# Order of reuse of SBUF buffers: the age of a release in ticks instead of in releases

## The chip, the cores and the metric

The kernel runs on one core of one Trainium2 chip. The metric is the device time of one execution in microseconds (us). A run repeats it and gives the median; two versions are compared by runs on the same chip.

## The reference

One inference step of a two-layer decoder in float32: 1024 prompt tokens and 8 decode tokens, model width 2048. Cut to what matters:

```
def pool_layer(x, prefix, pos, ...):                 # mixer A
    z = x @ w_in                                     # 2048 -> 4096
    u, gate = z[..., :D_POOL], z[..., D_POOL:]
    d, new_state = multiscale_pool(u, prefix, pos)   # trailing windows 2/4/8/16, minus u
    d = einsum('btgc,gce->btge', d, w_grp) * scale   # four groups of 512
    y = (d * silu(gate)) @ w_out
    return layer_norm(ALPHA * x + y), new_state

k, v = shared_kv(x)                                  # once, 4 KV heads of 64, partial rotary

def attn_layer(x, pos, kb, vb, ...):                 # mixer B
    z = x @ w_in
    q, gate = rope(z[..., :D_ATTN]), z[..., D_ATTN:]
    o = attn_core(q, kb, vb, ..., sinks)             # window 128, 32 heads, a sink per head
    y = (o * silu(gate)) @ w_out
    return layer_norm(ALPHA * x + y)
```

## The kernel before

**Tiling.** The tokens form two chunks (512 and 520 columns). The four big projections are the phases `ai`, `ao` (mixer A, in and out) and `bi`, `bo` (mixer B). Each phase treats its product as a two-by-two block product and needs, instead of eight block products, seven (`idx` 0 to 6) on sums of blocks, in the groups A (0, 5), C (1, 3, 6) and B (2, 4). Every operand is split in two: a high part rounded to fp32r, cast by ACT (weights L399, activations L613), and the rest, subtracted by DVE (weights L407, activations L619). PE then runs three matmuls for each 128 x 128 block, high by high, high by low and low by high (L784, L785, L786), of 260 or 512 columns. Sums of weight blocks are DVE's L443; some go to DRAM by POOL's queue and come back by SP's. L894, L896, L915, L924 and L954 move accumulators between PSUM and SBUF, POOL's L882 and L907 store parts of them, SP's L949 loads one part back. Between the projections stand the pooling, the attention (L1859 to L1987: scores L1880, mask L1900, exponentials L1915, transposes L1933, values L1962, the gate's activation L2028) and the layer norms.

**Ticks.** `plan` lists all units of work and gives each a tick; `self.i` is the tick that is being written, from -30 in the opening to some 800 at the end, and a tick holds 24 matmuls of 260 columns or 12 of 512. A load is put on the calendar 11 ticks ahead of its use (`L_LOAD`), a cast is due 5 ticks ahead, a subtraction 4 (`L_LOW`). Tasks without a fixed tick go when ACT and DVE have time by the planner's meters (`gentle`). `x_tick` starts loads of activations, and looks at how many buffers are free.

**Buffers.** `Mem` holds 53 SBUF buffers of 128 x 1040 floats, each usable whole or as two halves. `full` and `half` hand out the free one with the smallest number in `f`, which `release` wrote when the buffer came back. The number counts releases (`clock`, one more with each). A buffer whose content a DMA still has to store is given back at once with 10 added (`free(True)`), so that it is taken later. `half` takes a free half of a split buffer, unless that half came back within the last 6 releases and over 7 whole buffers are free; then it splits a whole one. The choice is made while the program is written: it sets no wait itself, but the new owner's first instruction waits on the chip until the old owner's last readers (engine or store) are done.

**Order.** `in_order` fixes the order of PE, ACT and DVE to that of the source. SP's loads and POOL's stores and memsets are ordered by the framework, and their place in the queue depends on the buffers that they take. Every queue runs in order: an instruction that waits holds all behind it.

Of the kernel before, what the change touches and what calls it, by code (L numbers as in the profile page):

```python
# [93 lines left out]
class Slot:  # L94


    def __init__(self, mem, i, h, a):
        self.mem, self.i, self.h, self.a = mem, i, h, a
# [9 lines left out]
        return self.r[:, : k * n].rearrange("p (k n) -> p k n", k=k)  # L108

    def free(self, stored=False):  # L110
        self.mem.release(self, 10 if stored else 0)


class Mem:


    def __init__(self, pool, n):
        self.pool = pool
        self.t = [None] * n
        self.f = [[0, 0] for _ in range(n)]  # L120
        self.clock = self.n = 0

    def new(self, i):
        self.n += 1
        self.t[i] = self.pool.tile([P, 2 * TMAX], F32, tag=f"m{i}", name=f"m{i}_{self.n}")
# [9 lines left out]

    def half(self):
        part = [(a if b is None else b, i) for i, (a, b) in enumerate(self.f) if (a is None) != (b is None)]
        if part and min(part)[0] > self.clock - 6 and len(self.whole()) > 7:
            part = []
        i = min(part)[1] if part else min(self.whole(), key=lambda i: max(self.f[i]))  # L140
        h = 0 if self.f[i][0] is not None else 1
        if not part:
            self.new(i)
        self.f[i][h] = None
        return Slot(self, i, h, self.t[i][:, h * TMAX : (h + 1) * TMAX])

    def release(self, s, late):
        self.clock += 1
        for h in (0, 1) if s.h is None else (s.h,):
            assert self.f[s.i][h] is None  # L150
            self.f[s.i][h] = self.clock + late


class Unit:
# [6 lines left out]
class Kern:  # L161
    def __init__(self, ctx, tc, io):
        self.tc, self.io = tc, io
        self.nc = tc.nc
        pool = lambda name, **kw: ctx.enter_context(tc.tile_pool(name=name, **kw))
        one = pool("one", bufs=1)
        self.smp = pool("smp", bufs=2)
        dram = pool("dram", bufs=1, space=bass.MemoryType.DRAM)
        self.psd = [pool(f"psd{i}", bufs=1, space=bass.MemoryType.PSUM) for i in range(3)]
        self.pso = pool("pso", bufs=1, space=bass.MemoryType.PSUM)  # L170
        self.four = None
        ctx.callback(self.use_four, None)
        self.prm = one.tile([P, N_PRM], F32, name="prm")
        self.cst = one.tile([P, N_CST], F32, name="cst")
        self.mki = one.tile([P, P], I32, name="mki")
        self.nsink = one.tile([P, NH], F32, name="nsink")
        self.carry = one.tile([P, NK, NST], F32, name="carry")
        self.kdec = one.tile([P, 2, NDEC], F32, name="kdec")
        self.qdt = one.tile([P, 256], F32, name="qd")
        self.qd = [  # L180
            self.qdt[:, i * P : (i + 1) * P].rearrange("p (b j t) -> p b j t", b=NDEC, j=2) for i in range(2)
        ]
        self.sgd = [one.tile([P, 8, NDEC], F32, name=f"sgd{i}") for i in range(2)]
        self.jr = one.tile([P, P], F32R, name="jr")[:]
        self.mem = Mem(pool("mem", bufs=1), NSLOT)
        self.n = self.ring = self.turns = 0
        self.lastO = -99
        self.i = -99
        self.cal, self.posts, self.side, self.tasks = {}, [], [], []
        self.seen, self.stepped, self.clock = 0, -9, {"p": 0.0, "v": 0.0, "a": 0.0}  # L190
        dr = lambda n, s: dram.tile(s, F32, tag=n, name=n)
        self.Td, self.act, self.n0, self.bb, self.ws = {}, {}, {}, {}, {}
        for ph in PH:
            n = INP[ph]
            self.Td[n] = dr(f"t{n}", [P, 8, 4, TMAX])
            for c in range(2):
                self.act[n, c] = io[f"x{c}"] if n == "x" else dr(f"{n}{c}", [P, NK, TMAX])
            self.n0[ph] = dr(f"n{ph}", [P, len(POS[ph]), TMAX])
            self.bb[ph] = dr(f"b{ph}", [P, len(POS[ph]), 2, TMAX])
            self.ws[ph] = [dr(f"s{ph}{p}", [P, 2, 1024]) for p in range(len(POS[ph]))]  # L200
        for c in range(2):
            self.act["p", c] = dr(f"p{c}", [P, NK, TMAX])
# [496 lines left out]
    def x_tick(self):  # L699
        free = lambda: len(self.mem.whole())  # L700
        n = 0
        for k in self.xl[:12]:
            far = self.x_at(k) - self.i
            if far > X_FAR or n > 1:
                break
            if self.x_ready(k, X_LAG if k[1] not in TROW and far > X_URGE else 0) and (
                (len(self.xraw) < 4 and free() > X_SPARE + 2) or (far <= X_LOAD and free() > 3) or far <= X_LOAD - 4
            ):
                self.x_load(k)
                n += 1  # L710
# [1776 lines left out]
```

## Time and profile before

| what | value |
|---|---|
| time, median of three runs | 2275.03 us (2274.45 to 2277.27) |
| the profiled execution's own time | 2273.81 us |
| its span, first to last instruction | 2272.0 us |
| mean granted PE clock | 0.999 |
| matmuls | 17312 |
| read from and written to HBM | 371.88 and 171.16 MB |
| loads of weights (L384, L435), 512 KB each, median from issue to landing | 5.0 to 7.0 us |

An engine's busy time is the time in which it executes; issuing a DMA or waiting is not counted. A row of the timeline has the start in us, the time in us, engine, line, operation and tiles; `x2` merges two that follow each other, and square brackets give the engine's idle time before and what ended it. SPq is SP's queue of DMA issues. In the trace's names the buffers' numbers are left out: `m` is any of the 53.

### The profile page before, as it was taken

Reading aid. Unit: us, or ns where it says so; the run is one execution under the profiler, and the core shown is the slowest. Engines: PE = TensorE matmul, PEld = TensorE weight load, DVE = VectorE, ACT = ScalarE, POOL = GpSimd, SP = SyncE. Lnnn points to the kernel's source line nnn. Section 1 sums busy time; section 2 is a strip of 40 time slices with the busy share of each in tenths; the row PEclk is TensorE's granted clock in tenths of the full one; section 3 lists DMA queues with packets and bytes.
Section 4 is the critical chain, followed back from the end, with each engine's and each line's share of the span. In section 5 each row is a group of like instructions: output and inputs, shape, how many; then the busy total and the mean of one; then the engine's idle time right before and its main releaser. Section 6 shows DMA issues by size and latency. Waiting matters only on the chain.

```text
span 2272.0 us, 42903 instructions
## 1 busy us (share of the span) xinstructions
PE 2262.4 (100%) x17312; PEld 2130.5 (94%) x17312; DVE 1598.4 (70%) x2009; ACT 1136.1 (50%) x2372; POOL 197.8 (9%) x418
## 2 busy tenths in 40 slices
PE   9999999999999999999999999999999999999998
PEld 7889999999999899999888899999999998889998
DVE  7667746746667587685786876666566879687688
ACT  6344333343334443454576644545647678553365
POOL 0101001100100111000011010101000000111000
PEclk9999999999999999999999999999999999999999
DMA  9859757673657898888488776666754556898873
GB/s 305 314 209 350 233 213 256 227 249 117 243 184 261 276 336 291 292 304 297 153 295 301 245 244 205 230 195 220 244 169 124 177 189 224 284 356 304 301 250 132
DMA packets 190262, 556.43 MB, mean 245 GB/s; under 512 B 26096, under 2 KB 31600, under 8 KB 190064
## 3 DMA queue, kind: packets, MB, share of 16 engines
q1 hardware_dynamic: 147936, 401.82, 54.0%
q0 software_dynamic: 41984, 151.61, 17.4%
q8 instruction: 135, 2.21, 0.4%
q14 instruction: 63, 0.52, 0.1%
q10 hardware_dynamic: 144, 0.27, 0.0%
HBM read 371.88 MB, written 171.16 MB: 239 GB/s over the span
## 4 chain that ended last, share of the span: by engine, by line
PE 96%; DVE 2%; ACT 1%; DMA 0%; issue 0%; SPq 0%; ACTq 0%; DVEq 0%
PE pD L784 28%; PE pD L786 28%; PE pD L785 28%; PE pD L1351 4%; PE pO L1962 2%; PE pS L1880 2%; PE pS L1933 1%; PE pD L848 1%; DVE m L619 0%; DMA m<-in_wia 0%; DVE m L407 0%; PE pO L848 0%; DMA m<-in_x 0%; PE pO L2087 0%; DVE m L1693 0%
## 5 line engine op out<-in xcount | busy, mean ns | idle before, releaser
L784 PE MATMUL pD<-m,m 128*128 128x260 f32 (+1 forms) x4736 | 1428.6, 302 | 0.4 <-ACT m L894 0.4
L786 PE MATMUL pD<-m,m 128*128 128x260 f32 (+1 forms) x4736 | 1420.7, 300 | 0.0
L785 PE MATMUL pD<-m,m 128*128 128x260 f32 (+1 forms) x4736 | 1420.2, 300 | 0.2 <-DVE m L619 0.2
L784 PEld LDWEIGHTS pD<-m,m 128*128 128x128 f32 x4736 | 891.7, 188 | 38.8 <-issue 5.5
L786 PEld LDWEIGHTS pD<-m,m 128*128 128x128 f32 x4736 | 891.4, 188 | 32.7
L785 PEld LDWEIGHTS pD<-m,m 128*128 128x128 f32 x4736 | 891.8, 188 | 31.9 <-DVE m L619 0.6
L407 DVE TENSOR_TENSOR m<-m,m 128x1024 fp32r<-128x1024 f32 x358 | 435.1, 1218 | 144.2 <-ACT m L399 118.9
L399 ACT CAST m<-m 128x1024 fp32r<-128x1024 f32 x358 | 373.0, 1045 | 48.4 <-DVE m L443 11.7
L443 DVE TENSOR_TENSOR m<-m,m 128x1024 f32<-128x1024 f32 x200 | 243.8, 1219 | 10.4 <-DMA m<-in_woa 2.5
L915 ACT COPY m<-pD 128x260 f32<-128x260 f32 (+1 forms) x126 | 56.0, 444 | 306.4 <-PE pD L786 306.0
L619 DVE TENSOR_TENSOR m<-m,m 128x1040 fp32r<-128x1040 f32 x108 | 130.0, 1234 | 24.1 <-ACT m L613 11.8
L924 ACT ACTIVATE m<-pD 128x260 f32<-128x260 f32 x100 | 38.7, 387 | 180.8 <-PE pD L786 172.7
L926 DVE TENSOR_TENSOR m<-pD,m 128x260 f32<-128x260 f32 x100 | 42.6, 426 | 113.0 <-PE pD L786 109.8
L613 ACT CAST m<-m 128x1040 fp32r<-128x1040 f32 x108 | 111.2, 1061 | 14.6 <-DVE m L407 6.7
L1915 ACT ACTIVATE m<-m,sm 128x128 f32<-128x128 f32 x256 | 99.2, 392 | 0.0
L1351 PE MATMUL pD<-m,m 128*128 128x260 f32 (+1 forms) x576 | 91.5, 319 | 0.0
L1351 PEld LDWEIGHTS pD<-m,m 128*128 128x128 f32 x576 | 82.0, 188 | 8.3
L896 ACT COPY m<-pD 128x260 f32<-128x260 f32 x68 | 25.6, 377 | 124.9 <-PE pD L786 124.9
L1945 DVE TENSOR_TENSOR m<-m,cst 128x1024 f32<-128x1024 f32 x32 | 39.1, 1221 | 69.0 <-ACT m L1941 68.7
L1928 ACT ACTIVATE m<-m,sm 128x128 f32<-128x128 f32 x256 | 81.8, 395 | 7.1 <-DVE sm L1923 7.1
L881 ACT ACTIVATE m<-pD 128x512 f32<-128x512 f32 x50 | 29.8, 597 | 99.4 <-PE pD L786 90.6
L894 ACT ACTIVATE m<-pD 128x260 f32<-128x260 f32 x68 | 26.4, 388 | 101.3 <-PE pD L786 101.3
(246 smaller groups left out, 1857.1 us busy)
## 6 DMA issues: line engine op xcount, KB each, us to landing
m<-in_wib SPq DMA_DIRECT2D x96, 512.0 KB, 5.0
m<-in_wia SPq DMA_DIRECT2D x94, 512.0 KB, 5.6
m<-in_woa SPq DMA_DIRECT2D x48, 512.0 KB, 6.2
m<-in_wob SPq DMA_DIRECT2D x48, 512.0 KB, 7.0
sbi<-m POOLq DMA_DIRECT2D x36, 512.0 KB, 4.2
m<-sbi SPq DMA_DIRECT2D x36, 512.0 KB, 4.5
m<-in_x SPq DMA_DIRECT2D x32, 520.0 KB, 7.4
sai<-m POOLq DMA_DIRECT2D x32, 512.0 KB, 3.9
```

The costliest lines, as they stand in the source:

```text
L399: self.nc.scalar.copy(e["hi"].r[:, :1024], e["raw"].a[:, :1024])
L407: self.nc.vector.tensor_sub(o.r[:, :1024], s.a[:, :1024], e["hi"].a[:, :1024])
L443: self.nc.vector.tensor_add(s[o].a[:, :1024], s[a].a[:, :1024], s[b].a[:, :1024])
L613: self.nc.scalar.copy(h.r[:, : 2 * TMAX], s.a[:, : 2 * TMAX])
L619: self.nc.vector.tensor_sub(o.r[:, : 2 * TMAX], s.a[:, : 2 * TMAX], h.a[:, : 2 * TMAX])
L784: nc.tensor.matmul(ps[:, :w], wh[:, s], h, start=new and n2 == 0, stop=False, skip_group_check=on)
L785: nc.tensor.matmul(ps[:, :w], wh[:, s], l, start=False, stop=False, skip_group_check=on)
L786: nc.tensor.matmul(ps[:, :w], wl[:, s], h, start=False, stop=n2 == 7, skip_group_check=on)
L915: self.evac(ph, pos)(self.dest(ph, pos, m, 0)(cs), ps[:, : cs.stop - cs.start])
L1351: nc.tensor.matmul(ps[:, : cs.stop - cs.start], ws[:, s], d[:, cs], start=f0 and k == 0, stop=l0 and k == 3,)
L1915: nc.scalar.activation(x["s3"][:, i, :], x["s3"][:, i, :], AF.Exp, bias=nm[:, i : i + 1], scale=0.125, accum_out=rs[:, i : i + 1],)
L1928: nc.scalar.activation(x["s3"][:, i, :], x["s3"][:, i, :], AF.Copy, scale=rs[:, i : i + 1])
```

## The change

A release is no longer numbered by the count of releases but by the tick in which it is written (`self.i`, which `Kern` hands to `Mem` as `tick`). `clock` now grows by 0.001 a release and only keeps the order within a tick. The handicap of a buffer that is still to be stored is 3.5 ticks instead of 10 releases; a half counts as fresh within 2 ticks instead of 6 releases. Before the first tick `tick` is negative, so buffers that come back in the opening now stand ahead of those never used, whose number is 0.

```diff
--- before.py
+++ after.py
@@ -108,7 +108,7 @@
         return self.r[:, : k * n].rearrange("p (k n) -> p k n", k=k)
 
     def free(self, stored=False):
-        self.mem.release(self, 10 if stored else 0)
+        self.mem.release(self, 3.5 if stored else 0)
 
 
 class Mem:
@@ -119,6 +119,7 @@
         self.t = [None] * n
         self.f = [[0, 0] for _ in range(n)]
         self.clock = self.n = 0
+        self.tick = lambda: 0
 
     def new(self, i):
         self.n += 1
@@ -135,7 +136,7 @@
 
     def half(self):
         part = [(a if b is None else b, i) for i, (a, b) in enumerate(self.f) if (a is None) != (b is None)]
-        if part and min(part)[0] > self.clock - 6 and len(self.whole()) > 7:
+        if part and min(part)[0] > self.tick() + self.clock - 2 and len(self.whole()) > 7:
             part = []
         i = min(part)[1] if part else min(self.whole(), key=lambda i: max(self.f[i]))
         h = 0 if self.f[i][0] is not None else 1
@@ -145,10 +146,10 @@
         return Slot(self, i, h, self.t[i][:, h * TMAX : (h + 1) * TMAX])
 
     def release(self, s, late):
-        self.clock += 1
+        self.clock += 0.001
         for h in (0, 1) if s.h is None else (s.h,):
             assert self.f[s.i][h] is None
-            self.f[s.i][h] = self.clock + late
+            self.f[s.i][h] = self.tick() + self.clock + late
 
 
 class Unit:
@@ -183,6 +184,7 @@
         self.sgd = [one.tile([P, 8, NDEC], F32, name=f"sgd{i}") for i in range(2)]
         self.jr = one.tile([P, P], F32R, name="jr")[:]
         self.mem = Mem(pool("mem", bufs=1), NSLOT)
+        self.mem.tick = lambda: self.i
         self.n = self.ring = self.turns = 0
         self.lastO = -99
         self.i = -99
```

No engine gets an instruction more or less. PE's order is the same throughout. Lines of the changed file stand two lower down in what follows (L2028 is L2030). In a name such as `m47_1964_21174` 47 is the buffer, 1964 counts the whole buffers handed out, and the last number counts all tiles.

First place: ACT in the attention of the last phase, at 1900 to 1910 us of the trace; ahead of the change

```order
L1915 ACTIVATE m42_1945_21047,sm_2857_21097<-m42_1945_21047,sm_2855_21095 128x128 x4
L2028 ACTIVATE m52_1963_21173<-m8_1932_20782 128x1040
L1941 COPY m6_1965_21202<-pS_2248_11329 128x1024
L1915 ACTIVATE m42_1945_21047,sm_2857_21097<-m42_1945_21047,sm_2855_21095 128x128 x4
L399 CAST m4_1968_21212<-m14_1944_20972 128x1024
L1896 COPY m2_1971_21255<-pS_2248_11329 128x1024
```

and now

```order
L1917 ACTIVATE m30_1946_21048,sm_2857_21098<-m30_1946_21048,sm_2855_21096 128x128 x4
L2030 ACTIVATE m47_1964_21174<-m34_1933_20783 128x1040
L1943 COPY m35_1966_21203<-pS_2248_11329 128x1024
L1917 ACTIVATE m30_1946_21048,sm_2857_21098<-m30_1946_21048,sm_2855_21096 128x128 x4
L401 CAST m10_1969_21213<-m37_1945_20973 128x1024
L1898 COPY m41_1972_21256<-pS_2248_11329 128x1024
```

with these rows of DVE at the same place of the changed program:

```order
L621 TENSOR_TENSOR m7_1955_21117<-m49_1886_20173,m26_1905_20437 128x1040
L621 TENSOR_TENSOR m38_1956_21119<-m47_1925_20708,m19_1948_21056 128x1040
L928 TENSOR_TENSOR m39_1940_20911<-pD_2847_20913,m31_1922_20702 128x260
L1865 TENSOR_TENSOR m36_1953_21108<-m35_1898_20330,m36_1953_21108 128x512
L409 TENSOR_TENSOR m9_1961_21168<-m33_1929_20751,m15_1942_20935 128x1024
L621 TENSOR_TENSOR m46_1962_21170<-m51_1931_20755,m42_1957_21121 128x1040
L621 TENSOR_TENSOR m49_1963_21172<-m10_1932_20757,m0_1958_21123 128x1040
```

The order is the same; L2030 (before L2028) now writes buffer 47, which the subtraction L621 into buffer 38 reads, and the cast L401 (before L399) writes buffer 10, read by L621 into buffer 49.

Second place: ACT some 90 us on, at 1993 to 2005 us, where attention tiles are split for `bo`. `qd` holds the decode columns that L611 copies into a tile ahead of its cast; ahead of the change

```order
L613 CAST m22_2064_22113<-m38_2033_21859 128x1040
L399 CAST m42_2066_22131<-m3_2048_22043 128x1024
L915 COPY m46_2059_22102<-pD_2912_21976 128x512
L611 COPY m0_2047_21993<-qd_81 128x2x8
L613 CAST m40_2068_22152<-m0_2047_21993 128x1040
L881 ACTIVATE m23_2072_22187<-pD_2922_22156 128x512
L1433 ACTIVATE m2_2075_22197<-m46_2059_22102 128x1024
```

and now

```order
L615 CAST m8_2066_22115<-m11_2035_21861 128x1040
L613 COPY m1_2047_21977<-qd_81 128x2x8
L615 CAST m31_2067_22118<-m1_2047_21977 128x1040
L401 CAST m44_2069_22136<-m25_2050_22045 128x1024
L917 COPY m37_2061_22104<-pD_2912_21979 128x512
L883 ACTIVATE m11_2071_22154<-pD_2922_22159 128x512
L1435 ACTIVATE m16_2077_22199<-m37_2061_22104 128x1024
```

The pair of copy and cast that stood behind the weight's cast (L399, now L401) and the copy out of PSUM (L915, now L917) stands ahead of them.

Third place: SP's queue from 1985 to 2008 us. `in_wob` are weights, `to` are sums of attention tiles, `h0` and `h1` are the residual of the two chunks, `nbo` is a stored part of an accumulator; ahead of the change

```order
L435 DMA m35_2060_22104<-in_wob 128x1024
L1379 DMA m37_2070_22169<-h0_121 128x2x512
L949 DMA m10_1951_21101<-nbo_146 128x520
L435 DMA m34_2073_22191<-in_wob 128x1024
L603 DMA m13_2078_22203<-to_143 128x2x512
L603 DMA m52_2069_22154<-to_143 128x2x512
L435 DMA m47_2074_22193<-in_wob 128x1024
L603 DMA m43_2092_22263<-to_143 128x2x512
L960 DMA m30_2079_22218<-h1_122 128x2x520
L435 DMA m45_2080_22220<-in_wob 128x1024
L603 DMA m1_2084_22231<-to_143 128x2x512
L603 DMA m7_2085_22233<-to_143 128x2x512
```

and now

```order
L437 DMA m29_2062_22106<-in_wob 128x1024
L605 DMA m15_2072_22157<-to_143 128x2x512
L1381 DMA m43_2073_22172<-h0_121 128x2x512
L951 DMA m11_2071_22154<-nbo_146 128x520
L437 DMA m10_2075_22193<-in_wob 128x1024
L437 DMA m6_2076_22195<-in_wob 128x1024
L962 DMA m12_2081_22220<-h1_122 128x2x520
L605 DMA m25_2080_22205<-to_143 128x2x512
L437 DMA m50_2082_22222<-in_wob 128x1024
L605 DMA m7_2085_22230<-to_143 128x2x512
L605 DMA m19_2086_22232<-to_143 128x2x512
L437 DMA m38_2087_22249<-in_wob 128x1024
```

One load of `to` (now into buffer 15) has moved ahead of those of `h0` and `nbo`, another (buffer 25) from ahead of weights and `h1` to behind them, and a third, which wrote buffer 43 ahead of the change, has gone behind these rows.

## Prediction

> **What bounds the kernel now.** I read the page first (busy shares, chain of waits), then PE's own waits, then a table of stretches, then the order of the changed program against the trace.
>
> ```profile
> span 2272.0 us, 42903 instructions
> PE 2262.4 (100%) x17312; PEld 2130.5 (94%) x17312; DVE 1598.4 (70%) x2009; ACT 1136.1 (50%) x2372; POOL 197.8 (9%) x418
> PE 96%; DVE 2%; ACT 1%; DMA 0%; issue 0%; SPq 0%; ACTq 0%; DVEq 0%
> ```
>
> PE is busy for 2262.4 of 2272.0 us, and it makes 96% of the chain that ended last. Nothing in this change takes a matmul away or adds one, so what it can give is bounded by the 9.6 us in which PE idles. Where these lie is in the table of stretches (each row: length, then busy us and count of each engine, granted clock, DMA share, GB/s), and what ended the longest of them is in the list of PE's waits (total, times, longest):
>
> ```profile
> 0.00:57.00 57.00, 54.83 (x233) 43.94 (x234) 44.34 (x60) 34.12 (x49) 5.03 (x23) 1.00 0.92 305
> 57.00:1881.00 1824.00, 1822.95 (x14107) 1725.65 (x14106) 1248.63 (x1554) 888.94 (x1898) 159.77 (x334) 1.00 0.70 239
> 1881.00:1938.00 57.00, 56.92 (x463) 50.28 (x461) 49.81 (x73) 48.30 (x134) 5.39 (x11) 1.00 0.66 227
> 1938.00:1995.00 57.00, 56.71 (x393) 46.12 (x393) 35.47 (x56) 29.98 (x70) 7.27 (x14) 0.97 0.84 292
> 1995.00:2052.00 57.00, 57.00 (x373) 52.09 (x372) 52.89 (x53) 26.86 (x41) 7.10 (x14) 1.00 0.97 343
> 2052.00:2109.00 57.00, 57.00 (x478) 57.00 (x477) 43.09 (x48) 19.90 (x32) 7.38 (x13) 1.00 0.87 300
> ...
> 2215.00:2272.00 57.00, 50.99 (x395) 49.63 (x393) 46.98 (x84) 32.77 (x65) 0.00 (x0) 0.99 0.37 133
> ```
>
> ```profile
> PE pO L2198 <- POOL m L880: 1.0, 1, 1.0
> PE pD L735 <- ACT m L2234: 0.7, 1, 0.7
> PE pO L1807 <- ACT m L924: 0.5, 1, 0.5
> PE pD L784 <- ACT m L894: 0.4, 1, 0.4
> PE pO L1962 <- DVE m L2108: 0.3, 1, 0.3
> ```
>
> 57.00 - 54.83 = 2.2 us are the opening and 57.00 - 50.99 = 6.0 us the closing normalisation. Between 57 and 2215 us PE idles 1.05 + 0.08 + 0.29 = 1.4 us in all. The waits behind that are for the copy of an accumulator, an attention value, a decode column: none is a wait for a buffer. So today the buffers cost PE nothing, and a better order of reuse has 1.4 us to win.
>
> **The change, part by part.** First, its size. The second number in a buffer's name counts the whole buffers handed out; the cast that the trace has at 1994.6 us writes the 2069th (second place shown with the change). That is 2069 / 1994.6 = 1.04 per us, and about as many come back, so ten releases, the old handicap of a stored buffer, are some 9.6 us. A tick is 24 matmuls of 260 columns; the row from 2052 us above gives 57 / 478 = 0.119 us for one, so a tick is 2.9 us and 3.5 ticks are 10 us (estimates from these rows). On average the two rules say the same; they differ where releases come in bursts.
>
> Instructions added or removed: none on any engine. What moves is (1) which buffer each instruction takes, hence which earlier reader it waits for; (2) the place of some twenty ACT and eight DVE instructions between 1994 and 2029 us; (3) the order of SP and POOL. I took each wait of the changed order and looked up in this trace whether the awaited reader had ended when the waiting instruction started. PE has no wait that would be late. Some ACT instructions, one group on DVE and some SP loads have. The largest of each kind follow.
>
> (1a) The gate's activation at 1902 us (first place shown with the change). It now writes buffer 47, which the second split of the DVE pair at L619 still reads.
>
> ```profile
> 1902.36 1.07 ACT L2028 ACTIVATE m<-m 128x1040 f32<-128x1040 f32 x1
> 1903.33 1.00 ACT L1941 COPY m<-pS 128x1024 f32<-128x1024 f32 x1
> ...
> 1905.77 1.04 ACT L399 CAST m<-m 128x1024 fp32r<-128x1024 f32 x1
> 1908.67 1.02 ACT L1896 COPY m<-pS 128x1024 f32<-128x1024 f32 x1 [1.85 <-PE pS L1880]
> ...
> 1901.82 2.39 DVE L619 TENSOR_TENSOR m<-m,m 128x1040 fp32r<-128x1040 f32 x2
> ...
> 1906.20 2.39 DVE L619 TENSOR_TENSOR m<-m,m 128x1040 fp32r<-128x1040 f32 x2
> 1908.84 1.21 DVE L1945 TENSOR_TENSOR m<-m,cst 128x1024 f32<-128x1024 f32 x1
> 1911.38 1.35 DVE L1900 COPY_PREDICATED m<-mki,pS 128x1024 f32<-128x1024 int32 x1
> ```
>
> The DVE pair ends at 1901.82 + 2.39 = 1904.21, so L2028 starts 1.85 us late. Behind it on ACT stand L1941 (then 1905.2 to 1906.2; DVE's L1945 needs it at 1908.84), four exponentials, and the cast L399. That cast writes buffer 10, read until 1906.20 + 2.39 = 1908.59 by the next DVE pair: 2.8 us late, ending at 1909.6. Behind it L1896 copies the scores, 1909.6 to 1910.6, and DVE's L1900 waits for it at 1911.38. The delay ends there with 0.8 us left: ACT's own idle 1.85 us before L1896 has taken it up. Cost 0; with that cover gone 2.8 us, and then one for one, since here DVE is the chain:
>
> ```profile
> 1887.78 0.60 DVE m L1863
> ...
> 1921.87 0.61 DVE m L1863
> 1922.53 1.45 PE pS L1880 x20
> ```
>
> (1b) The longest ACT wait for PE. The second of two casts at 2107.63 takes a buffer that a matmul of L785 reads until 2112.6.
>
> ```profile
> 2107.63 2.00 ACT L399 CAST m<-m 128x1024 fp32r<-128x1024 f32 x2
> 2121.43 0.38 ACT L915 COPY m<-pD 128x260 f32<-128x260 f32 x1 [11.80 <-PE pD L786]
> ...
> 2112.34 0.28 PE L785 MATMUL pD<-m,m 128*128 128x260 f32 x1
> ...
> 2120.03 1.22 DVE L407 TENSOR_TENSOR m<-m,m 128x1024 fp32r<-128x1024 f32 x1
> ```
>
> It would run from 2112.6 to 2113.7 instead of to 2109.6: 4.0 us late. Nothing stands behind it on ACT for 11.80 us, and its subtraction on DVE comes at 2120.03. Cost 0; cover left 6.3 us. The other ACT waits are shorter, with the same cover: casts are put in the plan ticks ahead of their use.
>
> (2) Among the moved pieces (second place) a copy and cast of an attention tile come before the cast L399 and the evacuation L915 instead of after them.
>
> ```profile
> 1998.49 0.59 ACT L915 COPY m<-pD 128x512 f32<-128x512 f32 x1 [2.83 <-PE pD L786]
> 1998.97 0.21 ACT L611 COPY m<-qd 128x16 f32<-128x16 f32 x1
> ```
>
> They need 0.21 + 1.06 = 1.3 us and ACT idles 2.83 us before L915. Cost 0; without that idle time L915 would be 1.3 us late.
>
> (3) SP's queue in the stretch with DMA share 0.97 (third place). The load of buffer 25 stood at 1995.32 and now comes just ahead of the load of L435 at 2006.57.
>
> ```profile
> 1995.32 0.88 SPq L603 DMA_DIRECT2D m<-to  x2
> ...
> 2006.57 0.58 SPq L435 DMA_DIRECT2D m<-in_wob  x1
> ...
> 2009.46 0.35 SPq L435 DMA_DIRECT2D m<-in_wob  x1
> ...
> 2015.93 1.23 DVE L443 TENSOR_TENSOR m<-m,m 128x1024 f32<-128x1024 f32 x1 [1.15 <-DMA m<-in_wob]
> 2021.10 1.23 DVE L443 TENSOR_TENSOR m<-m,m 128x1024 f32<-128x1024 f32 x1 [0.52 <-DMA m<-in_wob]
> ...
> 2024.53 1.23 DVE L619 TENSOR_TENSOR m<-m,m 128x1040 fp32r<-128x1040 f32 x1
> ...
> 2016.24 1.06 ACT L613 CAST m<-m 128x1040 fp32r<-128x1040 f32 x1
> ```
>
> Two loads here took 2015.9 - 2006.6 = 9.3 and 2021.1 - 2009.5 = 11.6 us to land. Issued at 2005 to 2006, buffer 25 lands between 2014.5 and 2017.6, for a cast at 2016.24: 0 to 1.4 us late. The subtraction that follows the cast stands on DVE at 2024.53, 7.2 us after the cast's end, so the cost is 0, and 1.4 us without that distance. The two L435 loads, for which DVE idled 1.15 and 0.52 us, get no later place: below nothing, down to -1.7 us of DVE time, which PE does not see (57.00 of 57.00 busy). POOL's order changes as well, but it is busy for 9% of the span; its stores are as many as before.
>
> The sum against the profiled execution: 2273.81 us (span 2272.0 and 1.81 around it) + 0 = 2273.8. The three runs have their median 1.2 us above that execution, so I forecast 2275.0 us. Within 0.2% of 2275.03 means 2270.5 to 2279.6, about what a measurement of this kernel can tell from no change.
>
> **Rivals.** *It wins the idle time.* If shifted loads also shorten the stalls inside the span, 1.4 us go: 2273.6. For it: the two DVE waits above. Against it: none of PE's waits is for a buffer. To pass 2270.5 it would have to win at the opening or the end as well, and the opening's waits (L2198, L735) are for a memset and the first casts.
>
> *SP blocked in the saturated stretch (slower).* SP runs in order; a load whose buffer is still read stops those behind it. Its longest such wait today is in this row:
>
> ```profile
> SPq L384 <- PE pD L786: 163.8, 48, 15.9
> ```
>
> Between 1995 and 2052 us DVE is busy for 52.89 of 57 us, so it can absorb 57 - 52.9 = 4.1 us; a wait of the kind shown beyond that reaches the splits and then PE. Worst, 15.9 - 4.1 = 11.8 us; in the middle about 6 us: 2281. It decides once a load of this stretch lands over 4.1 us later than its user wants it. For it: landings of 9 to 12 us, a late buffer 25. Against: the weight loads keep their places or gain. PE's clock shows one dip in the trace, 0.97 granted over the 57 us from 1938, or 1.7 us lost. The Trainium skill, "TensorE: Matmul & The Clock Gate", section "What's actually happening", says that the clock falls to half after an idle window of about 3.4 us, which speaks against any change that risks a long PE stall; no PE stall of that length stands in this trace to test it. By that rule this rival would end 1.7 us later, at 2283.
>
> *The change does nothing.* If the ages gave the same order, 2275.0 too; the order shows other buffers from the first loads on, so this is not the case as told, but the time is the same.
>
> **How the numbers follow.** Forecast 0.76 (own range 2273.0 to 2278.0: the 1.4 us of idle time with the spread of the runs below, 2.8 us for (1a) above), idle time won 0.11, of which 0.03 beyond 2270.5, SP blocked 0.13, of which 0.02 within 0.2%. So faster 0.03, same 0.76 + 0.08 + 0.02 = 0.86, slower 0.11. The range 2272.5 to 2280.0 adds to the upper side the 1.3 us of (2) and the first part of the SP case.
>
> **What would show it.** Right: PE busy within 1 us of 2262.4; no new PE wait over 0.5 us; L2028 after an idle ACT near 1904 us, ended by DVE L619; the cast at 2108 near 2112.6, ended by PE; L435's DVE waits near 2016 and 2021 shorter. Wrong: a PE gap behind L1880 near 1922 us (1a), behind L784 to L786 between 2015 and 2050 us (SP), or a second clock dip.

## The result, and the profile after

| kernel | median of runs | lowest to highest | runs | profiled execution | its span | mean PE clock |
|---|---|---|---|---|---|---|
| before | 2273.98 us | 2272.29 to 2277.27 | 20 | 2273.81 us | 2272.0 us | 0.999 |
| changed | 2280.10 us | 2273.46 to 2284.59 | 20 | 2280.35 us | 2278.6 us | 0.997 |

The ratio is 1.0026, with a 95% interval of 1.0020 to 1.0033: slower by some 6 us. The page of the changed kernel, its busy times and its chain:

```profile
span 2278.6 us, 42908 instructions
PE 2266.1 (99%) x17312; PEld 2133.2 (94%) x17312; DVE 1599.5 (70%) x2009; ACT 1135.5 (50%) x2372; POOL 197.4 (9%) x418
PE 95%; DVE 2%; DMA 1%; ACT 1%; issue 0%; SPq 0%; DVEq 0%; ACTq 0%
```

PE has the same matmuls but is busy 3.7 us longer, and idles 12.5 instead of 9.6 us; "DMA 1%" is new in the chain. The table of stretches of the changed kernel (columns as before) says where to look:

```profile
57.00:1881.00 1824.00, 1820.06 (x14060) 1722.58 (x14060) 1243.64 (x1546) 885.38 (x1891) 159.44 (x334) 1.00 0.70 238
1938.00:1995.00 57.00, 56.71 (x399) 46.52 (x398) 34.72 (x57) 28.56 (x71) 7.29 (x15) 0.94 0.79 275
1995.00:2052.00 57.00, 57.00 (x346) 50.65 (x346) 49.25 (x48) 30.92 (x47) 6.45 (x12) 1.00 0.95 345
```

The stretch from 1995 us, where the prediction saw the danger, is full as before. PE idles 3.9 instead of 1.05 us between 57 and 1881 us, and the clock is lower from 1938 us. PE's waits have one new row of weight, and the timeline of PE shows its place:

```profile
PE pS L1882 <- DVE m L1865: 2.7, 1, 2.7
```

```profile
1224.93 0.51 PE L1882 MATMUL pS<-m,m 64*128 64x256 f32 x4
1228.17 1.46 PE L1882 MATMUL pS<-m,m 64*128 64x256 f32 x20 [2.73 <-DVE m L1865]
1229.56 3.25 PE L1964 MATMUL pO<-m,m 128*64 128x128 f32 x28
```

The scores of an attention head wait for the low part of its queries (L1865, L1863 before the change). The values behind them (L1964) take 3.25 us for what takes 1.75 us in the kernel before, whose row is

```profile
1226.45 1.75 PE L1962 MATMUL pO<-m,m 128*64 128x128 f32 x28
```

PE runs at half clock. The clock's record changes in steps of 3.413 us, so the stretches are cut on that grid (columns as above, the clock third from the right):

```profile
1222.64:1226.05 3.41, 2.76 (x14) 1.80 (x12) 3.34 (x6) 3.41 (x5) 1.19 (x3) 1.00 0.38 157
1226.05:1229.46 3.41, 1.29 (x20) 1.24 (x20) 3.41 (x5) 0.74 (x1) 0.31 (x1) 1.00 0.88 284
1229.46:1232.88 3.42, 3.42 (x33) 2.99 (x29) 3.42 (x4) 3.21 (x4) 0.00 (x0) 0.50 1.01 366
1232.88:1236.29 3.41, 3.41 (x15) 2.78 (x16) 3.31 (x6) 0.84 (x2) 0.00 (x0) 1.00 0.08 29
```

Matmul by matmul against the kernel before, the changed one is level until 1225 us, 3.1 us behind after this wait, and 4.6 us behind after the window at half clock. Another 1.6 us come at 1938 to 1950 us, where the half clock behind the narrow matmuls of the decode scores lasts 6.8 us instead of 3.4; 0.4 us lie in small pieces. That is the 6.6 us between the spans. The 1.6 us cannot be put down to the change: in the ten other profiles with the same row of narrow matmuls the half clock behind it lasts 0, 3.4 or 6.8 us.

Back from the wait: DVE is late because it stood still for a transfer. DVE's rows of the kernel before, then of the changed one:

```profile
1216.37 0.69 DVE L1709 TENSOR_TENSOR m<-m,m 128x512 f32<-128x512 f32 x1 [3.64 <-DMA m<-m]
...
1223.94 0.68 DVE L1863 TENSOR_TENSOR m<-m,m 128x512 fp32r<-128x512 f32 x1
```

```profile
1219.86 0.69 DVE L1711 TENSOR_TENSOR m<-m,m 128x512 f32<-128x512 f32 x1 [7.17 <-DMA m<-m]
...
1227.43 0.68 DVE L1865 TENSOR_TENSOR m<-m,m 128x512 fp32r<-128x512 f32 x1
```

From the rope (L1709, now L1711) on, DVE works without a gap in both, so 3.49 us at the rope are 3.49 us at the scores. The transfer is `partner`: four DMAs of SP that swap quarters of 32 partitions of the queries for the rope. SP's issues of the kernel before, then of the changed one:

```profile
1191.54 0.33 SPq L384 DMA_DIRECT2D m<-in_wib  x1
...
1199.47 0.33 SPq L384 DMA_DIRECT2D m<-in_wib  x1
1201.62 0.38 SPq L603 DMA_DIRECT2D m<-th  x1
1203.20 0.33 SPq L1207 DMA_DIRECT2D h<-m  x1
1204.36 0.68 SPq L603 DMA_DIRECT2D m<-th  x1
1205.20 4.43 SPq L1703 DMA_DIRECT2D m<-m  x4
```

```profile
1191.51 0.37 SPq L605 DMA_DIRECT2D m<-th  x1
1194.40 0.33 SPq L1209 DMA_DIRECT2D h<-m  x1
1203.09 0.84 SPq L386 DMA_DIRECT2D m<-in_wib  x2
1204.02 0.40 SPq L1209 DMA_DIRECT2D h<-m  x1
1204.51 1.05 SPq L605 DMA_DIRECT2D m<-th  x1
1205.66 3.53 SPq L1705 DMA_DIRECT2D m<-m  x4
```

The load of weights that was issued at 1191.54 us now goes at 1203.09 us: its new buffer, 23, was still being stored to `th` until 1203.02 us, and SP waited 8.3 us for that store. A second load stood behind it. The quarters go only 0.46 us later than before, but behind two loads of weights, a store and a load of `th`, all issued within the last 2.6 us. The chain of waits of the changed kernel has the last of them:

```profile
1208.37 11.37 DMA m<-m
```

It lands at 1219.74 us, against 1216.25 us before the change.

### The profile page after: what moved, and what is told of

Same layout as the page of the kernel before. It is cut to its first block, busy times and chain, and to the rows that moved or that the text cites. A ratio compares the mean times of both kernels' runs of the same rounds, so it can differ in the third digit from the quotient of the medians.

```text
span 2278.6 us, 42908 instructions
## 1 busy us (share of the span) xinstructions
PE 2266.1 (99%) x17312; PEld 2133.2 (94%) x17312; DVE 1599.5 (70%) x2009; ACT 1135.5 (50%) x2372; POOL 197.4 (9%) x418
## 4 chain that ended last, share of the span: by engine, by line
PE 95%; DVE 2%; DMA 1%; ACT 1%; issue 0%; SPq 0%; DVEq 0%; ACTq 0%
PE pD L786 28%; PE pD L787 28%; PE pD L788 28%; PE pD L1353 4%; PE pO L1964 2%; PE pS L1882 2%; PE pS L1935 1%; PE pD L850 1%; DMA m<-m 0%; DMA m<-in_wia 0%; DVE m L621 0%; DMA m<-in_wib 0%; PE pO L850 0%; PE pO L2089 0%; DMA m<-in_x 0%
## 5 line engine op out<-in xcount | busy, mean ns | idle before, releaser
L401 ACT CAST m<-m 128x1024 fp32r<-128x1024 f32 x358 | 373.1, 1045 | 53.7 <-PE pD L787 14.5
L917 ACT COPY m<-pD 128x260 f32<-128x260 f32 (+1 forms) x126 | 55.9, 443 | 302.7 <-PE pD L788 298.5
L621 DVE TENSOR_TENSOR m<-m,m 128x1040 fp32r<-128x1040 f32 x108 | 129.9, 1234 | 13.8 <-ACT m L615 11.6
L883 ACT ACTIVATE m<-pD 128x512 f32<-128x512 f32 x50 | 29.8, 597 | 98.6 <-PE pD L788 90.3
```

Of the source, the lines that this page charges most:

```text
L401: self.nc.scalar.copy(e["hi"].r[:, :1024], e["raw"].a[:, :1024])
L621: self.nc.vector.tensor_sub(o.r[:, : 2 * TMAX], s.a[:, : 2 * TMAX], h.a[:, : 2 * TMAX])
L917: self.evac(ph, pos)(self.dest(ph, pos, m, 0)(cs), ps[:, : cs.stop - cs.start])
```

## The experiments

All against runs of the kernel before on the same chip (medians 2274.4 to 2274.7 us). The theory: **the held load**. It bunches SP's issues, the quarters land late, DVE and with it PE come late, and the clock halves. Its rivals: many small waits for other buffers; the clock alone; a handicap that is too short everywhere.

**One buffer given back.** `PICK` names the buffer for the n-th whole buffer handed out; here two choices swap their buffers and all others stay.

```diff
+PICK = {1306: 23, 1307: 24, 1308: 10}
     def full(self):
-        i = min(self.whole(), key=lambda i: max(self.f[i]))
+        i = PICK.get(self.n + 1, min(self.whole(), key=lambda i: max(self.f[i])))
```

(and the same in `half`, where a whole buffer is split)

> The changed kernel with one choice of buffer altered: the load of weights that waited for a store until 1203.1 us gets buffer 10, whose last reader ended at 1201.5 us, and buffer 23, which was being stored, goes to a DVE result that is first written at 1207 us. Nothing else moves but the name of these two buffers. Theory (the held load): SP issues the other load of weights near 1199.4 and this one near 1201.6 us instead of both at 1203.1 to 1203.9; the four quarter moves of the rope land near 1216.5 instead of 1219.7 us, PE's wait of 2.7 us at L1882 near 1225 falls below 0.5 us, the half-clock stretch of 3.413 us behind it is gone, and the time falls by 4.3 to 4.7 us from 2280.1, to about 2275.5. Rival (many small waits of ACT and DVE for other buffers, spread over the span): this one place is worth under 1 us, the time stays at 2279 to 2280. Rival (the clock alone: stretches at half clock come at random and the stall is their companion): a second stretch at half clock still shows somewhere between 57 and 1900 us, and the time stays above 2278.

Measured: 2274.10 us (2271.72 to 2277.44, 11 runs), ratio 1.0000 (0.9991 to 1.0008). SP, DVE and PE of this run (lines stand three lower than in the changed kernel):

```profile
1199.27 2.49 SPq L389 DMA_DIRECT2D m<-in_wib  x2
```

```profile
1217.73 0.69 DVE L1714 TENSOR_TENSOR m<-m,m 128x512 f32<-128x512 f32 x1 [5.18 <-DMA m<-m]
```

```profile
1226.04 1.45 PE L1885 MATMUL pS<-m,m 64*128 64x256 f32 x20 [0.85 <-DVE m L1868]
```

The whole loss is gone with one choice among more than 2000. That is 1.4 us more than the expectation counted for this place, and no run shows where this rest comes from. The quarters landed a little later than expected (1217.6 us), and PE still waits 0.85 us, but no half clock follows. The many small waits are out, since all but this one were still there.

**The load held in the kernel before.** The reverse, `PICK = {1305: 25, 1306: 20, 1307: 42, 1308: 7}` in the kernel before.

> The kernel before with one choice altered: the same load of weights, which SP issued at 1191.5 us, gets buffer 7, whose content a store has written only by 1202.7 us, and buffer 25 goes to the cast that had buffer 7 (ACT, 1206.7 us). Theory (the held load): SP stands until 1202.7 us, two loads of weights, one of th and the store of h1 are issued directly ahead of the four quarter moves, these land 3 us or more later than 1216.3 us, PE waits 2 to 4 us for L1863 (DVE) near 1225 us, a stretch of 3.413 us at half clock follows, and the time is 2278 to 2280. Rival (many small waits): the kernel before has none of them, so it stays at 2274 to 2275. Rival (the clock alone): a stall without a stretch at half clock, 2276 to 2277.

Measured: 2284.19 us (2282.32 to 2287.22, 5 runs), ratio 1.0045 (1.0032 to 1.0057). PE of this run at the place, and 690 us on, with ACT there:

```profile
1228.80 2.20 PE L1883 MATMUL pS<-m,m 64*128 64x256 f32 x20 [2.73 <-DVE m L1866]
...
1915.47 2.93 PE L1883 MATMUL pS<-m,m 64*128 64x256 f32 x24 [4.04 <-ACT m L1944]
```

```profile
1910.86 1.06 ACT L616 CAST m<-m 128x1040 fp32r<-128x1040 f32 x1 [5.73 <-DVE m L1866]
```

SP issued the load at 1199.85 us and not, as expected, at 1202.7, because the store that it waited for landed at 1199.80 us in this execution; the quarters still landed as late as 1220.37 us, 12.5 to 12.9 us after their issue. The stall is reproduced, 0.63 + 2.73 us with half clock behind it. The time is 4 us above the expected, by a second stall: the swapped names wander on, and at 1911 us a cast takes a buffer that DVE still reads, 5.73 us long, and holds the copy of the scores behind it on ACT. It is a wait of the kind of the prediction's (1a), too long for its cover.

**The quarters on ACT's queue.** In the changed kernel the four moves at this place alone are issued by ACT; the planner's meters do not see them, so nothing else moves.

```diff
+        eng = self.nc.scalar if self.mem.n == 1302 else self.nc.sync
+        self.meter()
-            self.nc.sync.dma_start(t.a[32 * a : 32 * a + 32, : n * T], s.a[32 * b : 32 * b + 32, : n * T])
+            eng.dma_start(t.a[32 * a : 32 * a + 32, : n * T], s.a[32 * b : 32 * b + 32, : n * T])
+        self.seen = len(self.nc.cur_bb.bb.instructions)
```

> The changed kernel with one thing altered: the four quarter moves at 1205.7 us are issued by ACT's queue instead of SP's; all buffers stay, and the load stays held until 1203.1 us. If what delays them is the backlog of SP's own queue (in the trace transfers of that queue land in the order of their issue, each about 2 us behind the one before: 1210.2, 1211.5, 1213.5, 1217.0, then the quarters at 1217.8 to 1219.7), they now land within about 5 us, by 1211, PE's wait at L1882 is gone and the time is about 2275.5. If it is the DMA engines as a whole (share 0.97 to 1.03 from 1204 to 1220 us), they land no earlier than 1216, and the time stays at 2278 to 2280.

Measured: 2277.80 us (2273.48 to 2281.11, 11 runs), ratio 1.0014 (1.0005 to 1.0023). Between the two. SP issued the load at 1204.7 us here. The first three quarters landed at 1211.5, 1213.4 and 1214.5 us, 6.8 to 8.5 us after their issue (some 5 had been expected; in the kernel before it is 7.7 to 8.9), while the load of `th` that SP issued at 1206.3 us landed at 1219.3 us, after 13.0 us. So most of the delay of these three is the backlog of SP's own queue. But the fourth was issued only at 1212.96 us, when the second load of weights had landed (1212.94 us), and ACT stood with it:

```profile
1204.74 8.73 ACTq L1707 DMA_DIRECT2D m<-m  x4
1213.52 0.21 ACT L1918 ACTIVATE sm<-sm 128x8 f32<-128x8 f32 x1 [8.81 <-DMA m<-m]
```

PE then waits 1.52 and 1.39 us for ACT (L883, L1933) instead of 2.73 us for DVE. The Trainium skill, "DMA: Bandwidth & Descriptors", section "Queues, rings and completion order", says that SP and ACT have rings of their own on the same DMA engines, which take turns between them; the three early landings agree.

**The handicap of a stored buffer.** The one number 3.5 in `free` is 6, 2, 3 and 4 ticks; and in the kernel before the 10 releases are 5.

```diff
-        self.mem.release(self, 3.5 if stored else 0)
+        self.mem.release(self, 6 if stored else 0)
```

> The changed kernel with the handicap of a stored buffer at 6 ticks instead of 3.5. From the held load: the buffer's value was released in tick 411, taken in tick 417, written by DVE at 1192.2 us and stored at 1203.0 us; at 2.9 us a tick 6 ticks are 17 us, which covers both the 6 us that DVE ran behind and the 10.8 us of the store. Theory (the handicap in ticks is too short): SP's waits for stores become fewer and shorter, the stall at 1225 us does not come, and the time is 2273.5 to 2276. Rival (ages in ticks are the fault, not the size of the handicap): a PE wait over 1 us for a DVE or DMA result remains somewhere between 57 and 2200 us, and the time is 2278 or more. All buffers change in this kernel, so a stall at another place would be neither.

> The changed kernel with the handicap of a stored buffer at 2 ticks, some 6 us, instead of 3.5. So far SP waited 439 us in all for stores and loads of other queues in the kernel before, 460 in the changed one and 422 with 6 ticks. Theory (the handicap is too short for what a store takes, 10.8 us at the place of the held load, and the stall was its consequence): still more such waits, 480 us or more, at least one PE wait over 2 us for a DVE or ACT result with a stretch at half clock behind it, and 2278 us or more. Rival (the stall at 1225 us was one unlucky meeting, and most waits of SP for stores cost PE nothing): more waits of SP too, but no PE wait over 1.5 us unless a load meets the quarter moves again, and 2273 to 2277 us.

> The kernel before, ages still counted in releases, with 5 added for a stored buffer instead of 10 (some 5 us). If the size of the handicap decides (theory), a PE wait over 2 us appears and the time is 2278 us or more, as in the changed kernel. If the stall is an unlucky meeting that any new order of buffers may or may not bring (rival), the time is 2273 to 2277 us, and the quarter moves at 1205 us, issued by SP behind three DMAs or fewer that have not landed, land by 1217.6 us as in the kernel before (1216.3) and in the run with the other buffer (1217.6).

> The changed kernel with 3 ticks for a stored buffer instead of 3.5. Waits of ACT and DVE for stores were 67 us in all with 2 ticks, 1.8 with 3.5, none with 6. Theory (two things: below some 3 ticks waits of ACT and DVE for stores come back and cost PE; above it only a single meeting of a held load with the quarter moves costs): 3 ticks stand at the edge, with 5 to 40 us of such waits and 2276 to 2286 us. Rival (the time falls evenly with the size of the handicap, 2288.8 at 2, 2280.1 at 3.5): 2283, with waits of SP that grow as well. Rival (only the meeting at 1225 us counts at any size): 2274 to 2276 if the quarter moves land by 1217.6 us, 2279 to 2281 if they land later than 1219.

> The changed kernel with 4 ticks for a stored buffer instead of 3.5. Theory (as for 3 ticks): waits of ACT and DVE for stores below 5 us in all; no PE wait over 1.6 us unless the quarter moves land later than 1219 us again; without that 2273.5 to 2276. Rival (the time falls evenly with the size of the handicap): 2278 to 2279, with small PE waits at several places.

Measured, with the waits of ACT and DVE for stores (the rows of both engines' lists of waits added up) and PE's idle pieces over 0.6 us from 20 us to the closing normalisation:

| handicap | median (runs) | ratio (interval) | ACT, DVE for stores | PE idle pieces, us |
|---|---|---|---|---|
| 2 ticks | 2288.75 (4) | 1.0063 (1.0050 to 1.0077) | 67.4 us | 0.88, 2.37, 2.18, 0.84, 1.23, 1.07, 3.29 |
| 3 ticks | 2274.82 (10) | 1.0004 (0.9995 to 1.0014) | 24.4 us | 1.43 |
| 3.5 ticks (the change) | 2280.10 (20) | 1.0026 (1.0020 to 1.0033) | 1.8 us | 2.73 |
| 4 ticks | 2279.18 (11) | 1.0019 (1.0010 to 1.0028) | 2.7 us | 2.01 |
| 6 ticks | 2275.36 (11) | 1.0007 (0.9998 to 1.0016) | none | 1.21 |
| 5 releases | 2291.58 (4) | 1.0076 (1.0059 to 1.0092) | 41.0 us | 0.97, 1.82, 2.03, 3.64, 2.39 |
| 10 releases (before) | 2273.98 (20) | 1 | 11.7 us | none |

Two things are at work. With 2 ticks or 5 releases ACT and DVE take buffers that are still being stored, and stand until the store has landed. With 2 ticks, ACT's cast at 2234 us stands 7.17 us for a store of the output, the copy to PSUM (L979) behind it is late, and PE idles 3.29 us:

```profile
2226.69 0.37 ACT L979 COPY pD<-m 128x260 f32<-128x260 f32 x1
2234.24 1.04 ACT L401 CAST m<-m 128x1024 fp32r<-128x1024 f32 x1 [7.17 <-DMA out_y<-m]
2235.19 1.51 ACT L1208 ACTIVATE m<-m,prm 128x512 f32<-128x512 f32 x2
2236.61 0.37 ACT L979 COPY pD<-m 128x260 f32<-128x260 f32 x1
```

With 5 releases it is, among others, a pair of DVE's at 1915.28 us, 4.21 us late by a store of `to`, with 3.64 us of PE idle. But from 3 ticks on the time does not follow the handicap, and 3 ticks are no slower than before: there the single wait at 1226 us is the only idle piece of PE over 0.6 us, and it follows the landing of the quarters. Of the expectations, the theory missed 3 ticks (its 24.4 us of waits cost nothing) and, at 6 ticks, the wait itself: the quarters landed at 1219.20 us, little earlier than in the changed kernel, and PE still idled 1.40 us, but without half clock behind it. Both rivals fall: the even slope at 3 and at 6 ticks (at 4 ticks its 2278 to 2279 us came, with one wait instead of small ones at several places), and "only the meeting at any size" at 2 ticks and 5 releases. SP's own waits for stores alone say nothing about the time: 340 us in all with 2 ticks, 432 in the changed kernel, 416 before. (With its waits for loads of other queues it is 374 us with 2 ticks, where the theory expected 480 or more.)

In the profiles in which PE comes to this place undelayed and DVE's order is the old one, the first rope's start on DVE decides. In the six of them with a wait, PE goes on with the scores 8.30 to 8.31 us after that start; what PE waits differs a little more, since PE arrives at 1225.2 to 1226.1 us:

| kernel | rope starts on DVE | PE waits at the scores | half clock behind it |
|---|---|---|---|
| decode in halves, before | 1214.92 us | 0 | no |
| before | 1216.37 us | 0 | no |
| decode in halves, one buffer given back | 1216.86 us | 0 | no |
| one buffer given back | 1217.73 us | 0.85 us | no |
| 3 ticks | 1218.89 us | 1.43 us | no |
| 6 ticks | 1219.33 us | 1.21 + 0.19 us | no |
| 4 ticks | 1219.45 us | 2.01 us | yes |
| changed | 1219.86 us | 2.73 us | yes |
| load held in before | 1220.49 us | 0.63 + 2.73 us | yes |

**DVE's order at the place.** In the changed kernel the rope of this pair of heads goes one tick later, so that the pooling (L1048 to L1051) stands ahead of it instead of behind.

```diff
-            self.at(3, lambda: b(0))
+            self.at(4 if (c, t0) == (0, 4) else 3, lambda: b(0))
```

> The changed kernel with the rope that waits for those four quarter moves one tick later in DVE's order: four pooling operations (L1048 to L1051, 2.6 us) and one subtraction of a weight now stand ahead of what waits for the transfer, or between its two halves, instead of all behind it. The held load stays held, and the quarters land as late as in the changed kernel (1219 to 1220 us). Theory (the late landing costs only through DVE's queue: what stands behind the waiting rope comes late): DVE does the pooling while the quarters are under way, L1865 starts near 1224.9 instead of 1227.4 us, PE's wait of 2.7 us at L1882 falls to 0.5 us or less, the half clock behind it is gone, and the time is 2275 to 2276.5. Rival (PE's wait has another cause that only comes with the held load, such as the second load of weights, or a DMA share near 1.0 that slows everything): the wait stays above 2 us and the time at 2279 to 2281.

Measured: 2275.69 us (2271.34 to 2279.39, 11 runs), ratio 1.0001 (0.9992 to 1.0010); PE's wait is gone. DVE of this run:

```profile
1212.36 0.65 DVE L1048 TENSOR_TENSOR m<-m,m 128x520 f32<-128x520 f32 x1
...
1217.75 0.69 DVE L1711 TENSOR_TENSOR m<-m,m 128x512 f32<-128x512 f32 x1 [2.79 <-DMA m<-m]
...
1222.75 0.68 DVE L1865 TENSOR_TENSOR m<-m,m 128x512 fp32r<-128x512 f32 x1
```

The load is held as long (SP issues it at 1202.65 us), and the time is that of the kernel before. From rope to L1865 are 5.0 instead of 7.57 us: the reordering gives 2.6 us. The expectation missed the landing: 1217.63 us, 2.1 us earlier than in the changed kernel's profile. With a landing at 1219.74 us L1865 would have ended at 1225.5 us (worked out), close to PE's arrival. And at the landing of this execution the old order would have cost some 0.85 us of wait and no half clock, as in the kernel with one buffer given back (rope at 1217.73 us). So what the reordering is worth is shown by the time of the 11 runs, and not by this one profile.

**The clock.** In the kernel with the one buffer given back DVE repeats the subtraction ahead of the scores in the 16 heads of the first chunk, with the same result.

```diff
+STALL = {(0, t): n for t, n in enumerate((3, 4, 5, 6, 7, 8, 9, 10, 4, 5, 6, 7, 8, 5, 6, 7))}
+            for _ in range(STALL.get((c, t), 0) + 1):
                 nc.vector.tensor_sub(x["ql"], q[:, :TP], x["qh"].bitcast(F32))
```

(cut: lines that hide the repeats from the planner's meters are left out)

> A measurement of the clock, on the changed kernel with the other buffer (the run of 2274.1 us, which has no stretch at half clock between the opening and the end): in the 16 heads of the first chunk DVE repeats the subtraction ahead of the scores 3 to 10 times (0.61 us each, the same result), so that PE waits there for some tenths of a us up to some 5 us. So far waits of 0.85, 1.2, 1.4 and 1.5 us had no half clock behind them, and waits of 2.7 and 4.0 us had one of 3.413 us. If a long idle time of PE alone brings the half clock, each wait over 2.7 us has such a stretch behind it and none below 2 us has; if the half clock comes at random, it does not follow the length of the wait. If it needs 3.4 us without a matmul, waits of 2 to 3.3 us have none. The time is 2273 us plus the waits, plus 1.7 us for each stretch at half clock.

Measured: one execution of 2322.52 us, with 34.0 us of such waits. Two of them, on the clock's grid (columns as above):

```profile
1485.77:1489.18 3.41, 1.79 (x16) 1.45 (x14) 3.27 (x6) 0.38 (x1) 0.63 (x2) 1.00 0.99 281
1489.18:1492.59 3.41, 1.44 (x22) 1.31 (x22) 3.34 (x5) 0.00 (x0) 0.48 (x1) 0.99 0.46 189
1492.59:1496.01 3.42, 3.42 (x31) 3.09 (x30) 2.64 (x3) 1.40 (x2) 0.06 (x1) 0.51 0.81 264
1530.14:1533.56 3.42, 1.82 (x16) 1.48 (x14) 3.25 (x6) 0.38 (x1) 0.00 (x0) 1.00 0.78 311
1533.56:1536.97 3.41, 2.71 (x44) 2.58 (x46) 2.06 (x3) 1.16 (x2) 0.00 (x0) 1.00 0.49 142
```

3.41 - 1.79 = 1.6 us of idle time in a window leave the next one at full clock, 3.41 - 1.44 = 2.0 us halve it; the wait of 2.30 us at 1532 us has no half clock behind it because the grid cuts it into 1.6 and 0.7 us. By their lengths the twelve waits of this run fit the first guess: the six of 3.59 to 5.44 us have half clock behind them, the six of 0.17 to 2.30 us have none. So it is not chance. But it is not the length alone either: the waits of 2.01 us with 4 ticks and of 1.82 us with 5 releases, each inside one window, have half clock behind them, and the 2.30 us here do not. By the same two waits, far less than 3.4 us without a matmul is enough.

**The decode scores in two halves.** Tried on the kernel with the one buffer given back and on the kernel before: `s0` does one half at tick D - 1, the other at D.

```diff
-            for pr in range(2):
-            (0, s0, 2), (1, s1, 3), (4, lambda: turn(x["st"]), 1), (5, s3, 3), (6, s4, 3), (7, s5, 3),
+            (-1, lambda: s0(0), 2), (0, lambda: s0(1), 2), (1, s1, 3), (4, lambda: turn(x["st"]), 1), (5, s3, 3), (6, s4, 3), (7, s5, 3),
```

(cut: the new body of `s0` is left out)

> A try for a version faster than both: the changed kernel with the other buffer, and the 32 matmuls of 16 columns for the decode scores (3.64 us near 1936 us, behind which the kernel before and most runs show a stretch of 3.4 or 6.8 us at half clock) in two halves of 16, one tick apart. If the long row of narrow matmuls brings the half clock there, the stretch is gone in the profile, and the median falls by up to 1.7 us below the run with the other buffer (2274.1), to 2272.5 to 2273.5; if the half clock there has another cause, the time stays at 2274 and the stretch still shows in some executions.

> The kernel before, with the decode scores in two halves one tick apart. In ten profiles a window of 3.413 us in which PE idled for 1.82 us or more had half clock behind it, one with 1.61 us or less had none, except behind the long row of narrow matmuls, where PE is busy by the records and half clock follows in 7 of 9 profiles with the row undivided. If the narrow matmuls count as idle in the same way, halves of 1.8 us, one in each window, are at the edge: the stretch becomes rarer, the median falls by 0.5 to 1.7 us, to 2273 to 2274. If not, the time stays at 2274.4.

(Half clock followed the undivided row in 6 of those 9 profiles, not in 7.) Measured: 2273.32 us (11 runs), ratio 0.9995 (0.9986 to 1.0004), and 2273.02 us (2272.30 to 2274.96, 11 runs), ratio 0.9994 (0.9985 to 1.0003). Neither of the two profiles has half clock there, against 7 of the 12 with the row undivided. The medians lie where expected, but no gain over the kernel before is shown.

## Why the prediction was wrong

It forecast no change, 2275.0 us with 2272.5 to 2280.0; it came 2280.1. Three of its own signs stand against it: PE is busy 3.7 us longer than 2262.4 us, PE has a new wait of 2.73 us, and the clock has a second dip. By its own steps:

**What bounds the kernel: right.** PE's busy time sets the end, and nothing tried went more than 1.4 us below the kernel before.

**The size: right on the average, and that was not the question.** Ten releases and 3.5 ticks are alike in the mean, and waits of ACT and DVE for stores even fell, from 11.7 to 1.8 us. What counted was one buffer.

**(1a) and (1b): right.** The two waits came as worked out, 1.86 for 1.85 us and 4.02 for 4.0 us, and cost PE nothing. ACT of the changed kernel:

```profile
1909.00 1.08 ACT L2030 ACTIVATE m<-m 128x1040 f32<-128x1040 f32 x1 [1.86 <-DVE m L621]
...
2119.31 1.05 ACT L401 CAST m<-m 128x1024 fp32r<-128x1024 f32 x1 [4.02 <-PE pD L787]
```

**(2): right**, no wait of PE there.

**(3) is the step that failed, with the way in which all waits were looked up.** The sum put every late load of SP at 0. Each wait of the changed order was compared with the landing times of the old trace, as if a DMA took as long behind another queue of loads. That DVE's waits for the loads of L435 (L437 now) would both shrink was wrong already by this: they are 3.50 and 0.23 us (at 2021.70 and 2027.73 us) where they were 1.15 and 0.52, hidden as said. And SP was examined only where the table of stretches showed a DMA share of 0.97. The row from 57 to 1881 us shows 0.70, but it is a mean over 1824 us; cut finer, the kernel before has this in it:

```profile
1180.00:1204.00 24.00, 24.00 (x147) 19.61 (x146) 17.54 (x23) 17.11 (x35) 4.85 (x11) 1.00 0.98 353
1204.00:1212.00 8.00, 8.00 (x36) 6.51 (x35) 6.23 (x10) 5.01 (x19) 2.17 (x4) 1.00 0.98 374
1212.00:1220.00 8.00, 8.00 (x40) 6.59 (x39) 3.96 (x8) 5.85 (x14) 0.55 (x1) 1.00 1.03 372
```

The 11.6 us by which the load of 1191.5 us comes later do no harm to its own user, so by the prediction's measure (how late does a load come for who uses it) they cost 0. They cost what was issued close behind: the quarter moves, for which DVE idled 3.64 us already before the change. DVE then had 0.6 us left: L1863 ended at 1224.62 us, and PE needed it near 1225.2 us. 3.49 - 0.6 = 2.9 us would have been the term, and 2.73 us came; with the half clock behind it the place cost 4.6 us, where the sum had 0.

**The rival "SP blocked": its mechanism, another place.** SP did stop, a landing came late, and PE waited for DVE; but at 1191 to 1228 us, not at 1995 to 2052, and its point of decision, 4.1 us of late landing, was taken from DVE's idle time in that stretch. Its price, 2281 to 2283 us, was near by luck, since it was worked out from the longest wait of SP and DVE's idle time elsewhere; its chance of 0.13 was too low, since it was weighed at one stretch alone.

**The clock.** The rival counted 1.7 us for a stretch at half clock only if PE stalls some 3.4 us. A window with 2.12 us of idle time had the same effect (1.5 us, 4.6 - 3.1). The rule that was weighed, the Trainium skill, "TensorE: Matmul & The Clock Gate", section "What's actually happening", speaks of one idle window of about 3.4 us that runs freely. The grid of 3.413 us agrees with every profile, but "idle" means here, by these runs, that something over half of it is (1.82 of 3.413 us are enough, 1.61 are not).

Shown by experiment: that the one choice of buffer makes the stall and the half clock behind it, and that its undoing takes the loss away; that with another order of DVE at the place the loss is gone too, while the load is held as before; that a window's idle time decides the clock. Only argued: why the landing of the quarters moves by up to 2 us between executions of like kernels, which is the likeliest cause of the wide spread of the changed kernel's runs (11 us, against 5 before). Of the 6.1 us between the medians the place explains 4.6; where the rest lies in the median run stays open. No version was found that is shown faster than the kernel before, and whether ages in ticks have a merit of their own stays open: with 3 and 6 ticks the interval holds 1.

## What to carry to other kernels

When a change reorders buffers or loads, do not price a late load by its own user alone: ask what stands close behind it on the same queue, and find in the trace of before the transfers for which an engine idles already, since these have no cover. Cut the table of stretches finely enough that a saturated stretch of 40 us is not averaged away. Changing which of 53 buffers is used can cost nothing (2274.8 us with 3 ticks) or several us by one unlucky meeting (2280.1 us with 3.5), so such a change is to be judged by its waits, one by one, and by several neighbouring settings, not by one.

## What the hardware showed that was not expected

In the profiles of the two kernels and the twelve experiments, of all windows of the 3.413 us grid at full clock that were followed by another, outside the opening, the end and the decode row, the 16 in which PE idled 1.82 us or more had half clock behind them and those with 1.61 us or less had none (both edges are from the run with 5 releases, in the windows from 830.4 and 2038.7 us). One window at half clock cost 1.5 us at the place of the held load and 1.6 us in the decode row, so a PE wait just past this edge costs nearly double: the profiled executions with waits of 1.43 us (3 ticks) and 2.01 us (4 ticks) at the same place, neither with half clock behind the decode row, took 2274.2 and 2276.6 us. A row of 32 matmuls of 16 columns, which the records show as 3.6 to 4.5 us of busy PE, is followed by half clock for one or two windows in 7 of 12 profiles, though the records show no idle time there.

On SP's queue a DMA's time from issue to landing followed what stood ahead of it more than its own size: in the changed kernel a quarter of 32 partitions took 11.4 to 12.1 us behind four others, and the two loads of weights of 512 KB ahead of them 7.1 and 8.0 us. In the kernel before the quarters took 7.7 to 8.9 us, and three of them on ACT's queue beside SP's backlog 6.8 to 8.5 us.
